# First head's values token by token, sample products in column strips, gates in one tile

## The chip, the cores and the metric

The kernel runs on one core of a Trainium2 chip. The metric is device time in microseconds of one launch; lower is better. The engines are called by their short names: PE multiplies matrices, DVE, ACT and POOL work on vectors, SP only issues transfers.

## What is computed

One inference step of a small hybrid layer: 512 new "prompt" frames without history and 32 "sample" frames that continue a stream with a stored state, 544 columns in all, model width 1024. The parts that matter here:

```python
xn = _rmsnorm(h, norm_g[l])
proj = xn @ w_in[l]
u, v_m, z_m, ig_pre, fg_pre, q_h, f_h, i_h, g_h, ga, gb = jnp.split(proj, _split_points(), axis=-1)
c = jax.nn.silu(_causal_conv(u, ...))            # 4 heads of 512 channels
qm, km = c @ w_qm, c @ w_km * M_HD ** -0.5       # per head
vm = v_m                                          # per head, 512 wide
ig, lf = ig_pre + b_ig, log_sigmoid(fg_pre + b_fg)
# mLSTM, per chunk and head
s = jnp.einsum('bhtd,bhsd->bhts', q, k) * dmat
num = w_inter[..., None] * jnp.einsum('bhed,bhtd->bhte', C, q) + jnp.einsum('bhts,bhse->bhte', s, v)
h = num / jnp.maximum(jnp.abs(den), jnp.exp(-m_t))[..., None]
C_new = decay[..., None, None] * C + jnp.einsum('bhs,bhse,bhsd->bhed', w_last, v, k)
...
hm = (_head_layernorm(h) + m_skip * c) * jax.nn.silu(z_m)
ya = hm @ w_brm
# a second branch (8 gated heads of 128), merge gates, w_out, and an output gate
```

The sample frames carry an old memory C (512 x 512 for each of the four heads); the prompt frames start from zero. Outputs are the layer's result and the new states of both streams, among them the memory C of each head (Cp for the prompt, Cs for the sample).

## The kernel before

**Precision.** An fp32 matrix is kept as a rounded high part and a rounded low part (fp32r), and a product is three PE instructions: high x high, low x high, high x low. The split of a weight is one copy (ACT, the high part) and one subtraction (DVE or POOL, the low part). Operands left as plain fp32 need one instruction for the exact product, which the profile shows as two records.

**Layout.** Work is feature-major: a tile has 128 features on the partitions and the 544 columns on the free axis, sample frames first, cut in two halves of 272. `dense` and `steps` go over the eight 128-row tiles of the contraction; with three parts and two halves, a unit of 128 output features is 48 PE instructions.

**The front.** PE first makes four units u (input of the convolution of head 0), then the two gates: `wg` has 36 columns, four at 0 for one gate and four at 32 for the other, and `steps(gp, wg, range(KD), 0, 36, 36)` is 48 products. Then `values()` makes four units v of head 0, with the low parts of their weights on POOL; each result is copied to a tile `vt`. Meanwhile DVE normalises x (`norm`, `norm_low`) and runs the convolution. The raw x and the raw weights stay in memory for a while; weights come in pieces of 512 columns, through a ring of eight raw buffers and a ring of five split pieces.

**The heads.** For each of the four heads in turn: keys (`stage_k`), queries (`stage_q`), scores (`stage_scores`: 512 x 512, and the sample's), then `mchain`, then the output projection (`stage_br`). `mchain` is a generator. It transposes the keys (blocks "kt", "kts"), loads the old memory c0 (four tiles), transposes the values (four blocks "vt" and the sample's "vts"), makes the new memory of the prompt (`memory`, tiles C, written out through Co), the numerators "nm" of the four row blocks, the numerators of the sample, the sample's new memory ("Cs", `new_memory`, eight pieces that are added to c0 by DVE), and the transposed result "yt". At each `yield n` it gives PE to a `Pump` for n steps of six instructions: the pump works through the input units that later stages need (z gates, values and u of the next head, the other branch's units) and prepares their weights a few pieces ahead. `EARLY` is the number of pump steps ahead of the first head's keys; a unit has eight.

**The sample block.** `old(f)` splits each of the four old memory tiles into high and low parts, and the query is split too. In `sample()` the query's high and low parts of several tiles stand side by side in the stationary operand (up to 128 columns), so that 18 products of 258 columns give the result in two strips of PSUM partitions, which are copied and added.

**The end.** The last head's new memory for the prompt does not lie in `mchain`: its operands go through DRAM, and `memories()` makes it at the very end of the kernel, in two PSUM banks of the other pool (`phalves`). The last tile's two copies to Co are followed by one transfer of the whole tile.

**Order.** The front's order on ACT, DVE and PE is the order of the code (`tc.manual_schedule`); after it only PE's is, and a scheduler places the instructions of the others; `tc.high_priority` and `tc.issue_after` move them ahead or hold them back. PSUM has eight banks: two two-bank buffers (`paux`) and four single ones (`pd`).

Of the kernel before, what the change touches and what calls it, by code (L numbers as in the profile page):

```python
# [46 lines left out]
AHEAD = 3  # L47
SCRATCH = 1024
# [3 lines left out]
EARLY = 8  # L52
# [12 lines left out]
def hybrid_step(ctx: ExitStack, tc: tile.TileContext, a, o):  # L65
# [69 lines left out]
    def weight(src, name, cols=1024, eng=V, chunk=WP):  # L135

        raws = [(raw_piece(src[:, c : min(c + WP, cols)], f"{name}r{c}"), min(WP, cols - c)) for c in range(0, cols, WP)]
        return [split_piece(r, f"{name}{i}", n, chunk, eng) for i, (r, n) in enumerate(raws)]

# [149 lines left out]
    cmask3 = cp.tile([3 * NS, NS], F32, name="cmask3")  # L289
    vone = cp.tile([3 * NS, 4], F32, name="vone")  # L290
# [557 lines left out]
    def stage_scores(h):  # L848

        dj, ds, wi, ks, ksm, qs, qf, qw = (st8[h][k] for k in ("dj", "ds", "wi", "ks", "ksm", "qs", "qf", "qw"))  # L850
        for i in range(KH):
            qt = small("qt", [P, NS])
            G.tensor_tensor(qt, qf[:, i * NS : (i + 1) * NS], wi, ALU.mult)
            G.tensor_copy(qw[:, i, 0], qt)
            G.tensor_tensor(qw[:, i, 1], qt, qw[:, i, 0].bitcast(F32), ALU.subtract)
# [40 lines left out]
    def memory(h, f, kw, vv, pool=paux):  # L896
# [16 lines left out]
        with tc.high_priority():  # L913
            for g in range(2):
                S.copy(co[:, g * VH : (g + 1) * VH], pn[g][:, :VH])  # L915
        nc.sync.dma_start(o["Cp"][h, f], co[:, :VW])
        yield

    kv_d = dr.tile([2 * NB, 2, P, VW], F32, name="kv_d")

    def mchain(h, pump):
# [23 lines left out]
        with tc.high_priority():  # L945
            S.mul(kws, pt[: 3 * NS, 0, :], wc)
            lo = slice(2 * NS, 3 * NS)
            V.scalar_tensor_tensor(kws[lo], pt[lo, 0, :], wc[lo], kws[lo].bitcast(F32), ALU.mult, ALU.subtract)
# [4 lines left out]
        def old(f):  # L953
            new = eslot if f < 2 else slot
            ch, cl = new(f"c0h{h}{f}", F32R), new(f"c0l{h}{f}", F32R)
            with tc.high_priority():
                S.copy(ch[:, :VW], c0[f][:, :VW])
                V.tensor_tensor(cl[:, :VW], c0[f][:, :VW], ch[:, :VW].bitcast(F32), ALU.subtract)
            return ch, cl


        if h:
            yield max(0, max(pump.when["v", f] for f in range(KH)) - pump.done)
        vt = t["vt"]
        vv = []
        for b in range(NB):
            yield 1
            pt = paux(f"vt{h}{b}")
            for f in range(KH):
                PE.transpose(pt[:, 0, f * P : (f + 1) * P], vt[f][:, NS + b * P : NS + (b + 1) * P], ident)  # L970
            if b < 2:
                vhl = sp.tile([P, 2, SLOT], F32R, tag="d", name=f"vhl{h}{b}", bufs=2)
# [937 lines left out]
```

## Time and profile before

| | |
|---|---|
| median of three runs | 1129.78 us (1127.34 to 1130.38) |
| the profiled execution | 1129.4 us, of which 1127.7 us are the span |
| PE busy | 1116.1 us (99%), 8849 records |
| DVE busy | 899.9 us (80%) |
| ACT busy | 682.4 us (61%) |
| POOL busy | 189.0 us (17%) |
| TensorE's granted clock | 1.0 throughout |
| memory traffic | 157.85 MB, 140 GB/s over the span |

A profile is one execution. Rows of the timeline and of the chain of waits have the start in us, the duration in us, the engine, the line, the operation with output and inputs, the size of the stationary operand (rows x columns) where it is a product, the shape, and the number of instructions in the row; a bracket behind tells a wait and what ended it. A record of PE is longer than the distance to the next one, because instructions overlap: distances are read from starts. In the view of waits a row gives the waiting operation, the releasing one, and then the total in us, the count and the longest. Groups give the count, the shape, and the lowest, middle and highest duration in ns, or the busy time with the mean, and then the idle time before. Rows of transfers end with the microseconds from issue to landing.

### The profile page before, as it was taken

The numbers are of one execution on the slowest core, as the hardware profiler recorded it, in microseconds if no ns is written. First come the engines' busy times: TensorE is split into PE (matmuls) and PEld (weight loads), VectorE is DVE, ScalarE is ACT, GpSimd is POOL, SyncE is SP. The second block draws the span as 40 slices with busy tenths as digits, with TensorE's granted clock in tenths as the row PEclk, the third lists the DMA queues.
The fourth block names the chain that finished last, engine by engine and source line by source line (L and its number), as shares of the span: only waits on it lengthen the run. The fifth ranks groups of instructions, "written<-read, shape, count | busy, mean of one in ns | idle before, by whom it ended". The sixth has DMA issues, their size and how long they took to land.

```text
span 1127.7 us, 24054 instructions
## 1 busy us (share of the span) xinstructions
PE 1116.1 (99%) x8849; PEld 1101.9 (98%) x8849; DVE 899.9 (80%) x2034; ACT 682.4 (61%) x1537; POOL 189.0 (17%) x356
## 2 busy tenths in 40 slices
PE   9999999999999999999999999999999999999998
PEld 9999999999999999999999999999999999999998
DVE  6886998576797786986888789999999977654585
ACT  5677657655666564665666477777776667332462
POOL 4842010100020100201000133232322210000000
PEclk9999999999999999999999999999999999999999
DMA  6133224323344142542667665666665685332743
GB/s 238 56 97 126 79 85 148 130 77 122 128 155 157 46 125 98 172 165 77 198 190 244 175 145 140 142 134 148 154 157 139 158 222 161 109 104 70 271 142 117
DMA packets 89997, 157.85 MB, mean 140 GB/s; under 512 B 10132, under 2 KB 17684, under 8 KB 89880
## 3 DMA queue, kind: packets, MB, share of 16 engines
q1 hardware_dynamic: 80928, 140.27, 38.4%
q0 software_dynamic: 8784, 15.99, 9.1%
q8 instruction: 69, 1.13, 0.4%
q14 instruction: 48, 0.39, 0.1%
q10 hardware_dynamic: 168, 0.06, 0.0%
HBM read 131.37 MB, written 24.91 MB: 139 GB/s over the span
## 4 chain that ended last, share of the span: by engine, by line
PE 85%; DVE 8%; DMA 3%; ACT 2%; issue 1%; POOL 0%; SPq 0%; ACTq 0%; DVEq 0%
PE d L485 35%; PE ya L151 9%; PE pg L1760 4%; PE q L151 4%; PE yb L151 4%; PE o L151 4%; PE C L903 4%; PE k L151 4%; PE sc L863 3%; PE pl L1532 2%; PE nm L1078 2%; DMA ws<-in_w_in 2%; PE ple L151 1%; DVE cv L634 1%; PE ht L1608 1%
## 5 line engine op out<-in xcount | busy, mean ns | idle before, releaser
L403 POOL DMA_DIRECT2D ws<-in_w_in x46 | 40.3, 877 | 239.9 <-DVE hkq L1556 36.7
L499 ACT COPY t<-d 128x272 f32<-128x272 f32 x126 | 47.8, 379 | 10.3 <-PE d L485 10.3
L1556 DVE TENSOR_TENSOR hkq<-hkq,q 128x288 f32<-128x288 f32 (+1 forms) x96 | 40.8, 432 | 3.5 <-ACT t L499 1.0
L634 DVE SCALAR_TENSOR_TENSOR cv<-ub,vec,cv 128x547 f32<-128x547 f32 x48 | 40.3, 840 | 1.7 <-ACT cv L629 1.4
L1532 PE MATMUL pl<-hkq,km 128*128 128x128 f32 x224 | 37.6, 290 | 1.3 <-ACT km L1521 1.2
L1532 PEld LDWEIGHTS pl<-hkq,km 128*128 128x128 f32 x224 | 31.2, 189 | 2.7 <-ACT km L1521 2.4
L1521 ACT COPY km<-hkq 128x256 f32<-128x256 f32 x56 | 24.0, 429 | 14.7 <-DVE hkq L1556 5.4
L1007 DVE SCALAR_TENSOR_TENSOR c<-c,wi,Cs 128x258 f32<-128x258 f32 x32 | 15.3, 479 | 20.1 <-PE Cs L1005 19.9
L915 ACT COPY Co<-C 128x258 f32<-128x258 f32 x32 | 10.4, 378 | 29.1 <-PE C L903 20.3
L1150 DVE TENSOR_TENSOR y<-ya,y 128x272 f32<-128x272 f32 x48 | 18.8, 434 | 8.8 <-PE ya L151 8.8
L1563 DVE COPY_PREDICATED at<-lmask,pl 128x256 f32<-128x256 uint8 (+1 forms) x56 | 25.2, 451 | 0.1
L626 POOL COPY uo<-ub 128x3 f32<-128x3 f32 x16 | 18.0, 1125 | 33.9 <-DVE ub L508 27.4
L1089 ACT COPY y<-nm 128x516 f32<-128x516 f32 x16 | 9.5, 591 | 21.6 <-PE nm L1078 21.6
L800 POOL COPY vsm<-vt 128x96 f32<-128x96 f32 x16 | 6.0, 384 | 88.2 <-ACT vt L510 44.7
L460 POOL DMA_DIRECT2D ws<-in_w_in x15 | 15.7, 1046 | 28.2 <-DVE ws272l L131 24.1
L1500 POOL TENSOR_SCALAR_AFFINE_SELECT aa<-at 128x128 f32<-128x128 f32 x32 | 18.4, 610 | 8.1 <-DVE at L1563 8.0
L1078 PE MATMUL nm<-vhl,sh 128*128 128x258 f32 x112 | 18.4, 286 | 0.0
L1037 DVE BATCH_NORM_STATS2 bs<-y 128x6 f32<-128x512 f32 (+1 forms) x20 | 13.7, 688 | 5.5 <-ACT y L1089 5.4
L979 POOL CAST vhl<-one 128x4 fp32r<-128x4 f32 x8 | 2.0, 245 | 95.8 <-PE nm L1078 95.8
L1747 DVE TENSOR_TENSOR h<-o,h 128x272 f32<-128x272 f32 x16 | 6.3, 436 | 14.5 <-PE o L151 14.5
L877 ACT CAST sh<-dm 128x512 fp32r<-128x512 f32 (+3 forms) x16 | 7.3, 459 | 16.6 <-DVE dm L871 16.6
L1662 ACT ACTIVATE osq<-kq 128x128 f32<-128x128 f32 x32 | 9.8, 305 | 12.4 <-DVE kq L1657 12.1
(4490 smaller groups left out, 5077.3 us busy)
## 6 DMA issues: line engine op xcount, KB each, us to landing
ws<-in_w_in POOLq DMA_DIRECT2D x61, 256.0 KB, 4.8
ws<-in_w_in SPq DMA_DIRECT2D x46, 256.0 KB, 3.8
ya_d<-y SPq DMA_DIRECT2D x32, 272.0 KB, 2.2
y<-ya_d SPq DMA_DIRECT2D x24, 272.0 KB, 3.8
c<-in_C SPq DMA_DIRECT2D x16, 258.0 KB, 4.0
out_Cp<-Co SPq DMA_DIRECT2D x16, 258.0 KB, 2.4
out_Cs<-c SPq DMA_DIRECT2D x16, 258.0 KB, 2.8
x<-in_xT SPq DMA_DIRECT2D x8, 272.5 KB, 4.8
```

The costliest lines, as they stand in the source:

```text
L151: PE.matmul(both[b][:m, :TH], part(w, off + k * step, m, x), xx[:, half(b)], start=(k == 0 and j == 0), stop=(k == n - 1 and j == 2),)
L403: G.dma_start(t, w_in[u][:, i * WP : (i + 1) * WP], accum_op=ALU.add)
L485: PE.matmul(ps, ww[:, c], xx, start=(start and k == 0 and j == 0), stop=end, skip_group_check=not start,)
L499: self.kept = S.copy(t, ps)
L634: V.scalar_tensor_tensor(cv[:, :547], ub[:, j : j + 547], vcol(V_CW + 4 * ft + j), cv[:, :547], ALU.mult, ALU.add)
L863: PE.matmul(pn[:, 0, :n], ks[f][x][:, j * P : (j + 1) * P], qs[f][y][:, NS + j * P : T], start=(f == 0 and i == 0), stop=(f == KH - 1 and ...
L903: PE.matmul(pn[g][:, :VH], kw[b][x][:, f * P : (f + 1) * P], vv[b][y][:, g * VH : (g + 1) * VH], start=(b == 0 and j == 0), stop=(b == NB ...
L1078: PE.matmul(pn[:, g, :VH], st[j][x][:, (i - j) * P : (i - j + 1) * P], vv[j][y][:, g * VH : (g + 1) * VH], start=(j == 0 and q == 0), stop ...
L1532: PE.matmul(pn[:, 0, b * P : (b + 1) * P], km[:, b * P : (b + 1) * P], view(qq, b * P, ((2 * c, P // (2 * c)), (HB + c, 2), (1, c))), star ...
L1556: V.tensor_tensor(x, x, d, ALU.mult)
L1563: V.copy_predicated(at[:, :n], lmask[:, li, :n], pn[:, 0, :n])
L1760: PE.matmul(ps, part(w, k * P, P, x), xx[:, c], start=(k == 0 and j == 0), stop=(k == KD - 1 and j == 2))
```

## The change

It has these parts.

- **Gates.** The gate weight is padded to 64 columns, and `gate_weight` builds one stationary tile of 100 columns out of it: the 64 rounded high ones and the 36 low ones. The high part of x meets all 100, the low part only the 36, so each of the eight contraction tiles takes two products for each half. The two gates come out in one tile `gt`, the low strip added by DVE.
- **Values of the first head.** They are made with the tokens on the partitions: x is the stationary operand (128 columns), the weight (512 columns, from a new arrangement `w_v` of the same numbers) the moving one; four PSUM banks `vp`, 96 products. The 32 sample rows are eight plain fp32 products `vq`: x times its norm weight (`xg`) against the raw weight, each in one of four strips of 32 output columns of PE, two deep. The row factor of the norm is applied by ACT and DVE as they read PSUM. So head 0 has no vt and vts transposes. The weights are split by ACT and DVE, not POOL, and DVE makes all low parts of x.
- **Sample block.** The query and c0 are used as plain fp32, without splits: for each half of the columns four products, one for each c0 tile, in four strips, and the product with the sample's own scores on top of the first. ACT copies one strip, DVE adds three. In the first three heads it stands ahead of the new memory; in the last one behind the first numerator block.
- **Memory.** The sample's new memory pieces are spread: one at each of four places in the numerators, the rest between pump steps of four ahead of yt. In the last head fewer pump steps stand before the first yt.
- **Front.** `EARLY` goes from 8 to 16: two z units ahead of the first keys. Small POOL operations are held behind one early sum (`issue_after(summed)`), sums `xf` are moved, the third convolution input is copied by ACT.
- **End.** The last memory tile is made, copied and sent by halves (`memory_halves`), on ACT's queue.

```diff
-EARLY = 8
+EARLY = 16
...
+    def gate_weight(src, name):
...
+            t = t[:, : n * (GW + GN)].rearrange("p (k c) -> p k c", k=n)
+            r = raw[:, i * n * GW : (i + 1) * n * GW].rearrange("p (k c) -> p k c", k=n)
+            S.copy(t[:, :, :GW], r)
+            V.tensor_tensor(t[:, :, GW:], r[:, :, :GN], t[:, :, :GN].bitcast(F32), ALU.subtract)
...
-            t.update(qs=[], qf=small("qf", [P, KH * NS]), qw=small("qw", [P, KH, 2, NS], F32R))
+            t.update(qs=[], qf=small("qf", [P, KH * NS]), qw=small("qw", [P, KH, NS]))
...
-    def memory(h, f, kw, vv, pool=paux):
+    def memory(h, f, kw, vv, pool=paux, after=None):
...
-        nc.sync.dma_start(o["Cp"][h, f], co[:, :VW])
+        (nc.scalar if pool is phalves else nc.sync).dma_start(o["Cp"][h, f], co[:, :VW])
...
+    def memory_halves(h, f, kw, vv, pn):
+
+        co = eslot(f"Co{h}{f}")
+        for g in range(2):
+            c = slice(g * VH, (g + 1) * VH)
...
+            S.copy(co[:, c], pn[g][:, :VH])
+            nc.scalar.dma_start(o["Cp"][h, f][:, c], co[:, c])
...
-        def old(f):
-            new = eslot if f < 2 else slot
-            ch, cl = new(f"c0h{h}{f}", F32R), new(f"c0l{h}{f}", F32R)
+        if h == 0:
+            vv, vs = t["vv"], t["vs"]
+        else:
...
-        yield 4
-        olds = [old(0), old(1)]
+                xf[1] = xf_sums(1)
+        yield 3
...
+        def sample():
+            pn = paux(f"nm{h}{NB}")
+            for g in range(2):
+                v = slice(g * VH, (g + 1) * VH)
+                for f in range(KH):
+                    PE.matmul(pn[f * NS : (f + 1) * NS, g, :VH], qw[:, f], c0[f][:, v], start=True, stop=f > 0)
+                PE.matmul(pn[:NS, g, :VH], dss, vs[:, v], start=False, stop=True)
+            ysm = eslot(f"y{h}{NB}")
+            with tc.high_priority():
+                first = S.copy(two(ysm[:, :VW]), pn[:, :, :VH])
+                for f in range(1, KH):
+                    last = V.tensor_tensor(
+                        two(ysm[:NS, :VW]), pn[f * NS : (f + 1) * NS, :, :VH], two(ysm[:NS, :VW]), ALU.add
+                    )
+            return ysm, first, last
...
-                if parts and i and (h == MH - 1 or i > 1):
+                if parts and (i, j) in ((1, 1), (2, 1), (3, 0), (3, 2)):
                     new_memory(*parts.pop(0))
...
+            if i == 0 and h == MH - 1:
+                ysm, *_ = sample()
+                numbers(NB, NS, ysm)
...
-            yield max(GAP if f == 0 else 1, pump.when["z", f] - pump.done)
+            while parts:
+                yield 4
+                new_memory(*parts.pop(0))
+            yield max(GAP - (16 if h == MH - 1 else 0) if f == 0 else 1, pump.when["z", f] - pump.done)
...
-            (V if k % 2 else G).tensor_tensor(xs[k][1], xt[k][:, :T], xs[k][0].bitcast(F32), ALU.subtract)
-
+            V.tensor_tensor(xs[k][1], xt[k][:, :T], xs[k][0].bitcast(F32), ALU.subtract)
...
-        steps(gp, wg, range(KD), 0, 36, 36)
...
+        vp = [pd.tile([P, 512], F32, tag="h", name=f"vp{b}") for b in range(NB)]
+        vq = paux("vq")
...
+            three = ((xh, wh), (xl, wh), (xh, wl))
+            for b in range(NB):
+                for j, (x, w) in enumerate(three):
+                    PE.matmul(
+                        vp[b],
+                        x[:, NS + b * P : NS + (b + 1) * P],
+                        w,
...
+            if k % NB == NB - 1:
+                for j in range(NB):
+                    i = k + 1 - NB + j
+                    PE.matmul(vq[j * NS : (j + 1) * NS, 0, :], xg[:, i], wraw[i], start=(i < NB), stop=(i >= NB))
...
+        def value_out():
...
+            c = r[:, b + 1 : b + 2]
+            S.mul(vh[:, :HD], vp[b], c)
+            V.scalar_tensor_tensor(vl[:, :HD], vp[b], c, vh[:, :HD].bitcast(F32), ALU.mult, ALU.subtract)
...
-        for f in range(KH):
+        for f in range(KH - 1):
             yield from memory(MH - 1, f, kw, vv, phalves)
+        memory_halves(MH - 1, KH - 1, kw, vv, phalves(f"C{MH - 1}{KH - 1}"))
+        yield
```

The first place is ACT between the end of the first head's values and the first keys, before. wi32 and wi33 are the weight pieces of the first two z units (two pieces each, 0 and 1), wk00 the first key weight, c and cs3h the convolved input, vt the values, z the z unit's silu.

```order
L1312 CAST cs2h<-c_905 128x544
L1303 COPY vt_915<-v_831 128x272
L1303 COPY vt_915<-v_832 128x272
L640 ACTIVATE c_968<-cv_667 128x32
L641 ACTIVATE c_968<-cv_667 128x512
L1312 CAST cs3h<-c_968 128x544
L130 CAST wi321h<-wi32r_893 128x512
L130 CAST wk000h<-wk00r_981 128x512
L130 CAST wk001h<-wk00r_983 128x512
L130 CAST wi330h<-wi33r_895 128x512
```

The same place on ACT in the changed kernel; vh are the value tiles, vp their PSUM banks.

```order
L1396 ACTIVATE vh_863<-vp_627,rms_r 128x512
L1396 ACTIVATE vh_869<-vp_628,rms_r 128x512
L657 ACTIVATE c_876<-cv_720 128x32
L658 ACTIVATE c_876<-cv_720 128x512
L688 ACTIVATE z_973<-z_973 128x544
L1381 CAST cs3h<-c_876 128x544
L132 CAST wi330h<-wi33r_818 128x512
L132 CAST wi331h<-wi33r_820 128x512
L132 CAST wk000h<-wk00r_895 128x512
L132 CAST wk001h<-wk00r_897 128x512
```

Before, the silu of the first z unit comes ten rows further down, behind wi330h and wi331h; now it stands ahead of cs3h and of the second unit's weights, and those stand ahead of the key weights.

The second place is PE at the sample block, before: the first seven of its eighteen products and the product with the sample's own scores (dss, vs). c0h and c0l are the parts of an old memory tile, qw the queries.

```order
L1055 MATMUL nm_2077<-c0h_1856,qw 128x258
L1055 MATMUL nm_2077<-c0l_1857,qw 32x258
L1055 MATMUL nm_2077<-c0h_1856,qw 128x258
L1055 MATMUL nm_2077<-c0l_1857,qw 32x258
L1055 MATMUL nm_2077<-c0h_1860,qw 64x258
L1055 MATMUL nm_2077<-c0l_1861,qw 32x258
L1055 MATMUL nm_2077<-c0h_1860,qw 64x258
...
L1052 MATMUL nm_2077<-vs,dss 32x258
```

The same block on PE now, whole; c are the four old memory tiles as loaded.

```order
L1041 MATMUL nm_1701<-c_1647,qw 32x258
L1041 MATMUL nm_1701<-c_1648,qw 32x258
L1041 MATMUL nm_1701<-c_1649,qw 32x258
L1041 MATMUL nm_1701<-c_1650,qw 32x258
L1042 MATMUL nm_1701<-vs,dss 32x258
L1041 MATMUL nm_1701<-c_1647,qw 32x258
L1041 MATMUL nm_1701<-c_1648,qw 32x258
L1041 MATMUL nm_1701<-c_1649,qw 32x258
L1041 MATMUL nm_1701<-c_1650,qw 32x258
L1042 MATMUL nm_1701<-vs,dss 32x258
```

Eighteen rounded products of 32 to 128 stationary columns became eight plain fp32 products and two rounded ones, all of 32.

More of the change, by code (lines that the diff above doesn't have):

```diff
@@ L1299, in values_out @@
[L1299 to L1306 removed]
+        norm_low(0)
+        with tc.issue_after(summed.ins):
+            uin.append(conv_in(3, acc[3], True))
+        value_weight()
+        cv = [conv_first(0, uin[0])]
+        gp = phalves("gates")
@@ L1356, in hybrid_step @@
             if h == 0:
+                with tc.issue_after(st8[0]["last"].ins):
+                    for k in (0, 3):
+                        xf[k] = xf_sums(k)
                 col, cols, combo = stage_cols(*rows)
```

309 lines of the change are left out of this document (175 added, 134 removed).

## The prediction

> **What bounds the kernel now.** First the page: which engine is full, and how much of the chain that ended last is its own.
>
> ```profile
> span 1127.7 us, 24054 instructions
> PE 1116.1 (99%) x8849; PEld 1101.9 (98%) x8849; DVE 899.9 (80%) x2034; ACT 682.4 (61%) x1537; POOL 189.0 (17%) x356
> PE 85%; DVE 8%; DMA 3%; ACT 2%; issue 1%; POOL 0%; SPq 0%; ACTq 0%; DVEq 0%
> ```
>
> TensorE (PE) is the bound. A busy share of 99% could hide gaps, since a record is longer than the step to the next one; so next the view of waits, for PE alone. All that it lists comes to 7 us:
>
> ```profile
> PE pl L1532 <- ACT km L1521: 1.2, 3, 0.7
> PE Cs L1005 <- DVE c L1007: 1.0, 3, 0.5
> PE vt L970 <- DVE vhl L978: 0.9, 1, 0.9
> PE yt L1120 <- DVE c L1128: 0.7, 1, 0.7
> PE r0pb L232 <- DVE rms_s L215: 0.3, 1, 0.3
> ```
>
> So the time is the number of PE steps times the step, plus a few waits. A change gains by taking steps off PE, and loses by new holes in PE. The steps are read from starts (timeline and chain), never from the length of a record:
>
> ```profile
> 177.79 24.16 PE ya L151 x192
> 227.38 0.40 PE L863 MATMUL sc<-qh,kh 128*128 128x512 f32 x1
> 230.16 0.34 PE L863 MATMUL sc<-qh,kh 128*128 128x384 f32 x1
> 33.98 0.66 PE L271 MATMUL gates<-x,wg0h 128*36 128x272 f32 x4
> 39.17 0.66 PE L271 MATMUL gates<-x,wg0h 128*36 128x272 f32 x4
> ```
>
> A rounded product with 272 columns costs 24.16/192 = 0.126 us. Between the 227.38 and the 230.16 row lie twelve products of 512 columns: 0.232 each. From the first gate row to the last named one are seven contraction tiles of six products: 5.19/42 = 0.124.
>
> **The change part by part.** *Gates:* 32 products instead of 48: -16 x 0.124 = -2.0 us.
>
> *First head's values, prompt:* 192 products of 272 columns go (-24.2), 96 of 512 come (+22.3): -1.9 us.
>
> *Values' transposes:* four blocks "vt" and one "vts" of the first head go.
>
> ```profile
> 117.26 0.41 PE L370 MATMUL d<-xh,wi340l 128*128 128x272 f32 x2
> 118.57 0.63 PE L970 MATMUL vt<-ident,vt 128*128 128x128 f32 x4 [0.89 <-DVE vhl L978]
> 118.95 0.50 PE L370 MATMUL d<-xh,wi340h 128*128 128x272 f32 x2
> 119.29 0.41 PE L370 MATMUL d<-xl,wi340h 128*128 128x272 f32 x2
> ```
>
> A block takes 118.95 - 118.57 = 0.38, and the pair of rounded products behind it 0.34 where 0.25 is usual: 0.47 a block, five blocks -2.4 us. The one long wait, 117.26 to 118.57 less 0.25, goes too: -1.1. But what DVE did there stays: preparing weights of the next units and the sums xu. Behind the scores DVE has six such operations of about 0.65 between its parts of the four kt blocks, so I expect kt and kts to wait about 1.2 in its place. Net: -2.3.
>
> *Sample values and sample strips.* Both use true f32 products, two PE records each, in four strips of 32 output partitions. Nothing in this trace has strips beside each other. The price of an f32 record, from a place with 128 columns:
>
> ```profile
> 667.83 1.05 PE L1627 MATMUL su<-hi,hkq 128*128 128x128 f32 x8
> 668.72 0.39 PE L1628 MATMUL su<-kit 128*128 128x128 f32 x2
> 668.86 0.37 PE L485 MATMUL d<-xh,wa1250h 128*128 128x272 f32 x1
> ```
>
> Eight records in 0.89 us: 0.111. That may be the weight load of 128 columns or the stream. If it is the stream, 258 columns cost 0.224 and 512 columns 0.444; if it is the load, 0.120 and 0.232 as for rounded ones. I take the dearer, since two passes per record fit the 0.111 either way, and keep the cheaper for the range. Before, the sample block is:
>
> ```profile
> 287.15 0.29 PE L1055 MATMUL nm<-c0h,qw 128*128 128x258 f32 x1
> 287.28 0.28 PE L1055 MATMUL nm<-c0l,qw 128*32 128x258 f32 x1
> 287.40 0.28 PE L1055 MATMUL nm<-c0h,qw 128*128 128x258 f32 x1
> 289.20 0.28 PE L1055 MATMUL nm<-c0h,qw 128*128 128x258 f32 x1
> 289.32 0.65 PE L1078 MATMUL nm<-vhl,sh 128*128 128x258 f32 x4
> ```
>
> 18 products in 2.17 us. After: per half four strips (8 records) and one rounded product. With strips side by side a half lasts as its one strip, 2 x 0.224, and the block 4 x 0.224 + 2 x 0.12 + 0.17 for two returns from f32 (0.085 each, as behind vt) = 1.3: -0.87 a head, -3.5 us. One record after the other it is 16 x 0.224 + 0.41 = 4.0, +1.8 a head. The eight sample value products cost 4 x 0.444 = +1.8 side by side, 16 x 0.444 = 7.1 in a row. I take side by side: each strip has weights and output partitions of its own.
>
> The rows 287.15 to 287.40 also show that going between 128 and 32 stationary columns costs nothing, 0.12 a step. The Trainium skill, "TensorEngine Tiling (Array Packing)", Key Properties, says that a change of tiling mode drains TensorE; by it the change would pay a drain at either end of each strip group, while here the trace disagrees at the first strip, and no row shows the others. The Trainium skill, "TensorE: Matmul & The Clock Gate", What overlaps and what doesn't, has matmuls in strict order of start and end, and measured 2.38 times the speed for three column tiles; by that the sample block would lie between my two ends.
>
> *What DVE and ACT do for it.* The splits of the old memory (a copy and a subtraction, sixteen of each) go; both engines have slack there, so nothing on PE is counted but half a microsecond of waits like yt's: -0.5. Two more additions of strips per head come on DVE (three for one), a PSUM buffer's release waiting on them:
>
> ```profile
> L993 DVE TENSOR_TENSOR vs<-vts,vs x4: 684/684/685, 121.2 to 566.9; 32x512 fp32r<-32x512 f32 x4
> L1089 ACT COPY y<-nm 128x516 f32<-128x516 f32 x16 | 9.5, 591 | 21.6 <-PE nm L1078 21.6
> ```
>
> 0.59 + 3 x 0.68 + hand-overs = 2.9 us. In heads 0 to 2 a pump step (0.76) and a memory product (24 x 0.12 = 2.9) run meanwhile. In the last head only nm1 does (12 products and one Cs, 1.6): PE waits +1.2. Spreading the Cs products takes the 1.0 of waits on c away. In the first head two old-memory tiles are loaded only behind the last kt block; three pump steps and the first strips cover all but +0.4.
>
> *The hole between the first two z units.* EARLY = 16 puts the second z unit ahead of the keys. Before, its first weight piece wi330h is copied on ACT ahead of the first unit's silu; now behind it, with cs3h between. PE needs wi330h, and the silu needs the first unit's end:
>
> ```profile
> 72.22 0.78 DVE L669 COPY z<-d 128x272 f32<-128x272 f32 x2
> 75.37 0.66 ACT L671 ACTIVATE z<-z 128x544 f32<-128x544 f32 x1
> 65.81 0.65 ACT L1312 CAST cs3h<-c 128x544 fp32r<-128x544 f32 x1
> 67.92 0.62 ACT L130 CAST wi330h<-wi33r 128x512 fp32r<-128x512 f32 x1
> ```
>
> 0.78 + 0.66 + 0.65 + 0.62 and 0.2 of hand-overs: PE stands still +2.9 us. Queued behind wi330h are wi331h and the first key weights, which then have a whole unit (6 us) of cover.
>
> *Start.* The second half of wu3 and the gate weights now stand behind the reciprocal root on DVE: r0pb's 0.3 goes. Two of the four value banks are the gates' own: they wait for two copies and additions behind DVE's norms, +0.6. DVE takes over the subtractions of the value weights and of x that POOL did beside it:
>
> ```profile
> 30.12 2.17 DVE L1255 SCALAR_TENSOR_TENSOR x<-x,rb 128x544 f32<-128x544 f32 x3
> 36.05 2.44 DVE L1255 SCALAR_TENSOR_TENSOR x<-x,rb 128x544 f32<-128x544 f32 x2
> ```
>
> 0.72 each at 30 us, 1.22 where POOL subtracts at the same time. With POOL idle, DVE at 0.7 keeps ahead: I count some 30 operations, 21 us, for the 25 us of value products that cover them. If that cover fails, rival 3 has the price.
>
> *Tail.* The last memory tile by halves:
>
> ```profile
> 1123.59 0.65 ACT L915 COPY Co<-C 128x258 f32<-128x258 f32 x2 [2.23 <-PE C L903]
> out_Cp<-Co SPq DMA_DIRECT2D x16, 258.0 KB, 2.4
> out_y<-h SPq DMA_DIRECT2D x16, 136.0 KB, 1.8
> ```
>
> One copy (0.38 for 0.65) and a transfer of half the size (1.8 for 2.4) stand behind PE's end: -0.9.
>
> *Sum:* -2.0 - 1.9 - 2.3 + 1.8 - 3.5 - 0.5 + 1.2 - 1.0 + 0.4 + 2.9 - 0.3 + 0.6 - 0.9 = -5.5 us. The profiled execution took 1129.4 (1127.7 of span and 1.7 around it), so 1123.9; the median of the runs, 1129.8, lies 0.4 higher: 1124.3.
>
> **The rivals.** *1. The strips chain* (the change does not quite do what it says). The two records of one f32 product use the same strip, so the second waits for the first, and in order of issue only it and the next strip's first overlap: five lengths for four strips. Sample values 10 x 0.444 = 4.4 (+2.6), sample block 9 x 0.224 + 0.41 = 2.4 (+1.1, four times): -5.5 + 2.6 + 4.4 = +1.5, 1131.3. For it: records come in pairs, and PE starts them in order. Against it: a cheap f32 record (0.120, 0.232) brings the same chain back to about 1125.
>
> *2. The strips do not overlap at all*, at the sample values and in every head: sample values +5.3 over my sum, blocks +2.7 four times: +10.6, 1140.4, slower. It decides once a block takes over about 3.6 us. For it: no row has two products at once. Against it: the separate output partitions.
>
> *3. The front starves.* DVE's operations stay at 1.2 instead of 0.7 while PE multiplies the first values; twelve operations more than fit, each 0.5, PE waits 6 us before z: +0.5, 1130.3; with the hole growing alike, 1133. For it: 36.05 above. Against it: POOL has only small copies left.
>
> **How the numbers follow.** The forecast's case 0.58, rival 1 0.24, rival 2 0.10, rival 3 0.08. A measurement of this kernel tells 0.3% from no change, 3.4 us. The first case is faster by more than that in nine of ten; rival 1 splits 0.2 faster, 0.5 the same, 0.3 slower; rival 2 is slower; rival 3 is 0.3 the same, else slower. Faster 0.52 + 0.05 = 0.57, same 0.06 + 0.12 + 0.02 = 0.20, slower 0.07 + 0.10 + 0.06 = 0.23. The range's lower end is my sum with cheap f32 records (-2.6) and no hole and no waits at kt (-4.1): -12.2, 1117.5. Its upper end is rivals 1 and 3 with 2.5 for unknown waits: 1134. Left out are rival 2 and the outer part of the others. The first case alone has 1118 to 1128.
>
> **What would show it.** In the profile after: the starts of the eight vq products and of a head's strips (1.3, 2.4 or 4.0 us a block decide between the cases); PE waiting on ACT wi330h for about 2.9; PE waiting on y in the last head for 1.2; vp products 0.232 apart without waits on DVE; the span ending about 3.2 behind PE's end. I am wrong if vp waits for its weights, if the keys start more than 4 us later than the removed and added products say, or if a strip block costs over 3.6.

## The result, and the profile after

The changed kernel takes 1135.62 us (median of five runs, 1134.34 to 1137.21), the kernel before 1129.78 (median of five too, 1127.34 to 1130.38): a ratio of 1.0057, 95% interval 1.0043 to 1.0072. It is slower by 6 us, where 5.5 us less were forecast. Each later ratio is to executions of the kernel before that were timed beside it, with medians between 1128.85 and 1129.23 us. The page and the cores' view (span and mean granted clock) of the changed kernel:

```profile
span 1133.3 us, 23757 instructions
PE 1112.4 (98%) x8733; PEld 1088.1 (96%) x8733; DVE 900.9 (79%) x2040; ACT 669.5 (59%) x1506; POOL 163.7 (14%) x308
PE 83%; DVE 5%; DMA 3%; ACT 2%; issue 1%; POOL 0%; ACTq 0%; POOLq 0%; DVEq 0%
core 0: 1133.3 us, clock 0.995
```

PE has 116 records fewer, and they are done later. Two things are new: a granted clock below 1, and in the waits of PE (waiting line, releaser, then us in total, count, longest) holes that before had no like:

```profile
PE C L917 <- ACT Co L929: 3.8, 1, 3.8
PE d L387 <- ACT wi330h L132: 2.5, 1, 2.5
PE k L167 <- POOL wk010l L133: 1.3, 1, 1.3
PE u L287 <- DVE wf2l L133: 1.3, 1, 1.3
PE nm L1094 <- ACT y L1105: 1.2, 2, 0.7
PE k L167 <- ACT wk010h L132: 1.0, 1, 1.0
```

Set side by side, the starts of PE's stages in the two timelines give a ledger (us):

| stretch of PE | before | after | after minus before |
|---|---|---|---|
| start of the gates | 33.98 | 35.24 | +1.3 |
| gates | 5.94 | 3.99 | -1.9 |
| values up to the first z | 24.09 | 25.13 | +1.0 |
| z units (one, now two) | 6.48 | 16.21 | +9.7 |
| first keys | 13.63 | 16.40 | +2.8 |
| rest of the first head, up to its "ya" | 93.51 | 90.49 | -3.0 |
| heads two, three, four | 428.11 | 423.89 | -4.2 |
| last "ya" to the last memory | 504.59 | 505.46 | +0.9 |
| last memory to the end of the span | 17.34 | 16.51 | -0.8 |

The second z unit (6.0 us) is only moved: it belongs to the rest of the first head, which so loses 3.0 and not gains. The first 188 us lose 9.8 us, the three later heads and the tail give 5.0 back, and 0.9 is lost in the long middle part, which has the same products before and after. In the profiles of this case that part takes 503.6 to 506.7 us, so 0.9 is within its spread.

### The profile page after: what moved, and what is told of

It reads as the page before. It is cut to its first block, busy times and chain, and to the rows that moved or that the text cites. A ratio compares the mean times of both kernels' runs of the same rounds, so it can differ in the third digit from the quotient of the medians.

```text
span 1133.3 us, 23757 instructions
## 1 busy us (share of the span) xinstructions
PE 1112.4 (98%) x8733; PEld 1088.1 (96%) x8733; DVE 900.9 (79%) x2040; ACT 669.5 (59%) x1506; POOL 163.7 (14%) x308
## 4 chain that ended last, share of the span: by engine, by line
PE 83%; DVE 5%; DMA 3%; ACT 2%; issue 1%; POOL 0%; ACTq 0%; POOLq 0%; DVEq 0%
PE d L502 34%; PE ya L167 8%; PE yb L167 4%; PE q L167 4%; PE o L167 4%; PE pg L1860 4%; PE k L167 4%; PE C L917 4%; PE sc L877 3%; PE nm L1094 3%; PE pl L1632 2%; DMA ws<-in_w_in 2%; PE ple L167 1%; PE yt L1142 1%; PE ht L1708 1%
## 5 line engine op out<-in xcount | busy, mean ns | idle before, releaser
L651 DVE SCALAR_TENSOR_TENSOR cv<-ub,vec,cv 128x547 f32<-128x547 f32 x48 | 37.5, 783 | 0.4
L917 PE MATMUL C<-vhl,kwh 128*128 128x258 f32 x96 | 16.5, 296 | 4.4 <-ACT Co L929 3.8
L917 PEld LDWEIGHTS C<-vhl,kwh 128*128 128x128 f32 x96 | 14.0, 201 | 4.7 <-ACT Co L929 4.0
L1094 PEld LDWEIGHTS nm<-vhl,sh 128*128 128x128 f32 x112 | 15.4, 190 | 2.0 <-ACT y L1105 1.7
```

Of the source, the lines that this page charges most:

```text
L651: V.scalar_tensor_tensor(cv[:, :547], ub[:, j : j + 547], vcol(V_CW + 4 * ft + j), cv[:, :547], ALU.mult, ALU.add)
L917: PE.matmul(pn[g][:, :VH], kw[b][x][:, f * P : (f + 1) * P], vv[b][y][:, g * VH : (g + 1) * VH], start=(b == 0 and j == 0), stop=(b == NB ...
L1094: PE.matmul(pn[:, g, :VH], st[j][x][:, (i - j) * P : (i - j + 1) * P], vv[j][y][:, g * VH : (g + 1) * VH], start=(j == 0 and q == 0), stop ...
```

## The experiments

**The hole at the memory.** The longest wait stands between the second and the third tile of the first head's new memory. First PE's timeline there, then ACT's:

```profile
137.07 0.28 PE L1027 MATMUL Cs<-vs,kws 96*128 96x258 f32 x1
141.17 1.23 PE L917 MATMUL C<-vhl,kwh 128*128 128x258 f32 x4 [3.82 <-ACT Co L929]
145.55 0.28 PE L1027 MATMUL Cs<-vs,kws 96*128 96x258 f32 x1
```

```profile
139.76 0.43 ACT L340 ACTIVATE xfh<-xv 128x272 fp32r<-128x272 f32 x1
140.47 0.65 ACT L929 COPY Co<-C 128x258 f32<-128x258 f32 x2 [0.28 <-DMA out_Cs<-c]
144.58 0.65 ACT L929 COPY Co<-C 128x258 f32<-128x258 f32 x2 [3.14 <-DMA out_Cp<-Co]
```

PSUM is not free because Co has not been copied; the copy's own releaser is a transfer that writes out an old-memory tile. Either the copy has no buffer until that tile is gone, or it stands behind the casts xfh in ACT's queue. By the code, the ring of twelve buffers ("e") then holds three z tiles, four value parts, four old-memory tiles and the sample's y. One edit frees a tile earlier and leaves the casts:

```diff
+            if h == 0:
+                new_memory(*parts.pop(0))
+                new_memory(*parts.pop(0))
             for f in range(KH):
                 for _ in memory(h, f, kw, vv, after=read):
```

> The changed kernel with one edit: in the first head two pieces of the sample's new memory (both halves of the first old-memory tile) stand ahead of the prompt's memory, so that this tile is written out and its buffer comes free earlier. Theory A (buffers): PE stands still 3.98 us at 137 us because the first Co has no free buffer until the first old-memory tile has been written out; with the edit that hole and the half clock behind it (1.5 us more) go, about -5 us, 1130.5. Rival B (order on ACT): Co stands behind the casts of the sums xf, which wait for DVE; DVE is as late as before, so the hole stays and the time is 1135.6 within 1.

1128.88 us, a ratio to the kernel before of 0.9993 (0.9983 to 1.0003). The first Co is copied at 133.1 us, and PE's stretch from the first C to "ya" falls from 57.07 to 51.06 us. Theory A holds: 6 us of the loss come from a missing buffer, the 4.0 us hole and the slow products behind it.

The products behind that hole are slow, too. The windows view (busy PE, count, granted clock, DMA share, GB/s) around the three long holes:

```profile
72.00:72.50 0.50, 0.00 (x0) 1.00 0.00 0
72.50:73.00 0.50, 0.00 (x0) 0.63 0.00 0
73.00:76.00 3.00, 2.84 (x12) 0.50 0.34 87
76.00:77.00 1.00, 1.00 (x10) 0.98 0.32 84
89.50:90.00 0.50, 0.11 (x1) 0.70 0.00 0
90.00:93.00 3.00, 3.00 (x13) 0.50 0.43 105
93.00:94.00 1.00, 1.00 (x9) 0.95 0.60 215
140.50:141.00 0.50, 0.00 (x0) 0.90 0.00 0
141.00:144.00 3.00, 2.83 (x13) 0.50 0.49 175
144.00:145.00 1.00, 1.00 (x9) 0.85 0.00 0
```

From the last half us of each hole the granted clock is half for 3.4 us: a mean of 0.63 over the first half us is 0.37 us at half clock, then come 3.0 and then 0.04, and the other two add up alike. In the kernel before, no hole was that long, and the clock was 1.0 until PE's last product. The Trainium skill, "TensorE: Matmul & The Clock Gate", Part 1, tells of such a gate, with free-running windows of 3.4 us. The traces agree on the length: ahead of PE's last product, every stretch at half clock in these runs lasts 3.4 us or twice that. The next run tests whether the idle time is the cause.

```diff
                 new_memory(*parts.pop(0))
+                if h == 0 and f == 1:
+                    fillp = pd.tile([P, 512], F32, tag="h", name="fillp")
+                    for _ in range(14):
+                        PE.matmul(fillp, kw[0][0][:, :P], vv[0][0][:, :512], start=True, stop=True)
```

> The changed kernel with fourteen products added in the memory's hole at 137 us (512 columns, 0.232 us each, 3.25 us in all, into a PSUM bank that nothing reads). They need only what is there, so they run while PE would wait for the first Co. Theory A (clock): the granted clock drops because PE stood still, and the 3.4 us at half speed behind the hole go once it is filled: the third memory tile's twenty-four products take 2.9 us instead of 4.5, the mean granted clock rises by about 0.0015, -1.5 us, 1134. Rival B: the slow stretch behind the hole is something else (transfers, weights, a refill of queues): no change, 1135.6, or longer where the products delay the memory.

1135.34 us, ratio 1.0049 (1.0036 to 1.0062): not to be told from the changed kernel's. PE's timeline, where fillp are the added products:

```profile
137.95 3.44 PE L1072 MATMUL fillp<-vhl,kwh 128*128 128x512 f32 x14
141.96 0.74 PE L917 MATMUL C<-vhl,kwh 128*128 128x258 f32 x4 [0.57 <-ACT Co L929]
144.96 0.28 PE L1027 MATMUL Cs<-vs,kws 96*128 96x258 f32 x1
146.11 0.75 PE L917 MATMUL C<-vhl,kwh 128*128 128x258 f32 x4 [0.87 <-ACT Co L929]
```

The clock stayed at 1.00, and the third tile's 24 products took 3.0 us for 4.4. All six kernels of this case that keep the hole, the changed one among them, show the half clock there, so the idle time is its cause. But the fourth tile now waits 1.0 us: each Co copy waits for the transfer of the one before it, as in ACT's rows above, and the slow clock had only hidden that wait. From the first C to the first "yt" it is 42.7 us for 42.8. Theory A is right on the clock and wrong on the time.

**The holes of the front.** Behind the hole of the z units, PE waits twice at the second key weight, wk010. PE's timeline, then ACT's ahead of that weight's copy, both in the changed kernel:

```profile
87.82 0.52 PE L167 MATMUL k<-cs0h,wk010h 128*128 128x272 f32 x2 [1.05 <-ACT wk010h L132]
89.89 0.60 PE L167 MATMUL k<-cs0h,wk010l 128*128 128x272 f32 x1 [1.30 <-POOL wk010l L133]
```

```profile
80.82 1.28 ACT L726 ACT_TABLE_LOAD   x1
82.79 1.28 ACT L688 ACT_TABLE_LOAD   x1
84.08 0.66 ACT L688 ACTIVATE z<-z 128x544 f32<-128x544 f32 x1
84.76 1.28 ACT L727 ACT_TABLE_LOAD   x1
87.17 0.60 ACT L132 CAST wk010h<-wk01r 128x512 fp32r<-128x512 f32 x1
```

The copy comes 6.6 us after the keys' start (80.57). In the kernel before it came 3.0 us after it (70.49), ahead of the silu and its table load:

```profile
73.45 0.60 ACT L130 CAST wk010h<-wk01r 128x512 fp32r<-128x512 f32 x1
```

Waits in the text are gaps between PE's starts less one step; the idle time in a row's bracket is 0.1 to 0.3 us shorter. Four edits follow, each on the changed kernel: the second z unit's first weight ahead of other work; the silu of the first z unit behind the key weights' copies; the second key weight at high priority; POOL's small copies no longer held behind the early sum.

```diff
         conv_rest(2, uin[2], cv[2])
-        silu_low(1)
         silu()
         conv_rest(3, uin[3], cv[3])
         value_out()
         value_out()
+        pump.prepare(5)
+        silu_low(1)
         silu_low(2)
         silu()
-        pump.prepare(5)
```

> The changed kernel with one edit: the first weight piece of the second z unit (wi330) is prepared ahead of the last convolved input and of the low parts cs1l and cs2l. Theory A: the hole between the first two z units (2.66 and 0.27 us of waiting, and 1.0 us of the half clock behind it) goes: -3.7 us, 1131.9. Rival B: DVE and ACT are the bound of this stretch, and what is won there is waited for again at the keys, whose weights come from the same queues: within 1 us of 1135.6, the keys' waits longer by 3 us.

```diff
-            act = S.activation(z[:, :T], z[:, :T], AF.Silu)
+            with tc.issue_after(made["wk001"][0].ins) if f == 0 else nullcontext():
+                act = S.activation(z[:, :T], z[:, :T], AF.Silu)
```

> The changed kernel with one edit: the silu of the first z unit is held behind the copy of the key weight wk001 on ACT, so that it no longer stands ahead of cs3h, wi330h, wi331h and wk000h. Theory A: the hole between the first two z units is ACT's order and nothing else; without the silu wi330h is copied about 1.9 us earlier, the wait falls from 2.66 to under 1 us, the clock stays full, and the silu falls behind the table loads of the gate rows so that one of them goes as well and the key waits shrink: -3 to -6 us in all, 1130 to 1132.5. Rival B: what is won is given back at the keys, as it was when only the weight was moved ahead: 1135 to 1143.

```diff
-            w = st8[h].pop("wk", None) or weight(a["w_km"][h, u], f"wk{h}{u}", eng=V if h else G)
+            with tc.high_priority() if u and not h else nullcontext():
+                w = st8[h].pop("wk", None) or weight(a["w_km"][h, u], f"wk{h}{u}", eng=V if h else G)
```

> The changed kernel with one edit: the second key weight is prepared with high priority, so that its copy on ACT stands ahead of a table load, a silu and the key copies. Theory A: the two key waits (1.21 and 1.46 us) and the half clock behind them (about 1.5 us) come from ACT's queue; -3 to -4 us, 1132. Rival B: POOL's subtractions of the low parts (1.3 to 2.0 us each) are the bound, and the second wait stays: -1 us, 1134.6.

```diff
-        with tc.issue_after(summed.ins):
-            uin = [conv_in(f, acc[f], False) for f in range(NF)]
+        uin = [conv_in(f, acc[f], False) for f in range(NF)]
...
-            with tc.issue_after(summed.ins):
-                G.tensor_copy(vh[:, HD:VW], one4)
-                G.tensor_copy(vl[:, HD:VW], zero4)
+            G.tensor_copy(vh[:, HD:VW], one4)
+            G.tensor_copy(vl[:, HD:VW], zero4)
```

> The changed kernel with one edit: the small copies on POOL are not held behind the early sum any more (xg still is), so that POOL's second addition of squares comes after them, as before the change. Theory A: this addition, beside DVE's subtraction of wf2, stretched that to 1.86 us from 0.55 and made PE wait 1.4 us; it goes: -1.3 us, 1134.3, wf2l at 0.6 us. Rival B: PE waits there for x and the first weights, which landed 0.6 us later in this execution: no change beyond 0.5 us.

| run | median, us | ratio to before (95%) | keys begin | first queries begin | scores begin |
|---|---|---|---|---|---|
| changed kernel | 1135.62 | 1.0057 (1.0043 to 1.0072) | 80.57 | 96.97 | 110.58 |
| z_weight_ahead | 1143.67 | 1.0134 (1.0109 to 1.0159) | 78.92 | 99.51 | 118.55 |
| z_silu_late | 1132.51 | 1.0032 (1.0020 to 1.0044) | 78.14 | 96.28 | 109.99 |
| key_weight_ahead | 1136.47 | 1.0064 (1.0042 to 1.0087) | 79.92 | 93.39 | 108.69 |
| pool_fill_free | 1133.43 | 1.0043 (1.0028 to 1.0058) | 77.99 | 96.95 | 110.58 |

The last three columns are PE's starts in the profiled executions. Each edit closed its own hole, and most of it was waited for again before the scores. z_weight_ahead lost more than it won: PE then waited for the key weight wk011 3.4 and 2.4 us, and for a query 3.0 us, and ran at half clock for 6.8 us behind the keys' waits and again behind the query's; what rival B names, and worse. In z_silu_late the wait for wi330h fell to 0.8 us as theory A has it, but the keys then waited 2.1 us for a PSUM bank, as rival B has it. In key_weight_ahead the second key wait went too, against its rival B; then PE waited 1.1 us for a bank and 1.4 us for a query weight, and the time is the changed kernel's. In pool_fill_free the wait for wf2l went, against its rival B, and the gates start 1.60 us earlier, but the first queries 0.02. So the local mechanism was right in all four, and the time followed it only in part. In pool_fill_free the keys begin 2.6 us earlier, and all of it is lost up to the first queries: PE waits 2.1 us for wk010h instead of 1.2, and the half clock behind the key waits lasts 6.8 us instead of 3.4. z_silu_late (at the edge of its theory A) and pool_fill_free (below its own) were timed 3 and 2 us faster than the changed kernel although their scores begin no more than 0.6 us earlier, but the interval of each touches that of the changed kernel. For z_silu_late its single executions give a likely reason: the profiled execution (1135.55 us) has two stretches of 6.8 us at half clock and a mean clock of 0.993, while the other four ran at 0.997 or 0.998 and took 1131.83 to 1132.74.

EARLY back at 8:

> The changed kernel with EARLY back at 8, the keys straight behind the first z unit. Theory A: the keys' weights stand behind the same silu and the same copies on ACT and then behind POOL's subtractions, so PE waits for the first key weight about 5 us instead of 2.7 for wi330h, and the second z unit no longer covers the rest: slower than the changed kernel by 2 to 5 us, 1137.5 to 1140.5. Rival B: the second z unit ahead of the keys is itself the harm, and the time goes back by the hole and its clock, -3.7, to 1132.

1129.60 us, ratio 1.0002 (0.9993 to 1.0011). Theory A had the front right: PE waits 3.7 us for the first key weight and 2.8 us for a query weight. It missed the memory: with one z tile less in the ring, the 4 us hole is not there, which shows the missing buffer a second time. Rival B's time is nearer, but not for the reason it gives, the hole between the z units and its clock.

**The strips.** PE's timeline of the sample block in the changed kernel, the four parts of each product merged:

```profile
128.12 0.64 PE L1041 MATMUL nm<-c,qw 128*32 128x258 f32 x8
128.69 0.30 PE L1042 MATMUL nm<-vs,dss 96*32 96x258 f32 x1
128.93 0.64 PE L1041 MATMUL nm<-c,qw 128*32 128x258 f32 x8
129.50 0.31 PE L1042 MATMUL nm<-vs,dss 96*32 96x258 f32 x1
129.65 0.41 PE L387 MATMUL d<-xh,wi350h 128*128 128x272 f32 x2
```

Eight records in 0.57 us; the block takes 1.53. To see what lying side by side is worth, all four products go to one strip, on the kernel with the buffer mended:

```diff
-                    PE.matmul(pn[f * NS : (f + 1) * NS, g, :VH], qw[:, f], c0[f][:, v], start=True, stop=f > 0)
+                    PE.matmul(pn[:NS, g, :VH], qw[:, f], c0[f][:, v], start=(f == 0), stop=False)
```

> The kernel of mem_two_ahead (1128.9), with the four old-memory products of each half of the sample block all in one strip of 32 columns, added up in PSUM, without DVE's additions. Theory A: the strips run side by side, and in one strip the sixteen records of a block follow each other at 0.111 to 0.24 us: a block takes 3.0 to 4.3 us for 1.6, four heads +6 to +10, less 1 us of waits for DVE's additions: 1134 to 1138. Rival B: the records would be as quick one after the other, and the strips only cost the additions: 1128 or less.

1137.10 us, ratio 1.0069 (1.0056 to 1.0083), 8 us more than mem_two_ahead. The same eight records:

```profile
127.93 1.93 PE L1041 MATMUL nm<-c,qw 128*32 128x258 f32 x8
129.79 0.31 PE L1042 MATMUL nm<-vs,dss 96*32 96x258 f32 x1
```

1.86 us for 0.57: four strips run 3.3 times as fast as one strip. Theory A holds.

**What is left when the holes are closed.** four_mended joins mem_two_ahead, z_silu_late, key_weight_ahead and pool_fill_free; key_copies_first adds high priority for the copies of the first keys out of PSUM; key_lows_on_DVE puts those key weights' subtractions on DVE; early_8_mended has EARLY 8 with the key and POOL edits alone.

> The changed kernel with four edits together: two pieces of the sample's new memory ahead, small POOL copies free, the second key weight at high priority, the first silu of z held back. Theory A: the holes were the whole loss (5.3 + 1.4 + 4 + 3.7 us of the span, some of it counted twice because a later wait takes it over): 1122 to 1126, faster than the kernel before by 4 to 7 us. Rival B: DVE, 90% busy from 60 to 100 us, is the bound of the front, so that only the memory's hole is won: 1128 to 1130.

> four_mended (1126.4) with the copies of the first keys out of PSUM at high priority, ahead of a table load and the gate rows on ACT. Theory A: PE's wait of 2.64 us for a PSUM bank at 83 us and the half clock behind it are this order on ACT; they go, part of it is waited for again at the next weight: -1.5 to -3 us, 1123.4 to 1125. Rival B: DVE and POOL are the bound, no change: 1126.4.

> key_copies_first with the subtractions of the first head's key weights on DVE, not POOL. While POOL subtracts (1.3 to 1.8 us each), DVE's operations of the same kind take 1.8 us instead of 0.69. Theory A: POOL's help costs DVE as much as it saves; with all four on DVE (4 x 0.69 = 2.8 us) DVE loses about 2.5 us of stretching and the weights are ready earlier: same as key_copies_first or up to 1.5 us faster. Rival B: DVE is full and four more operations delay all that stands behind them: +1 to +3 us over key_copies_first.

> The changed kernel with EARLY 8, small POOL copies free, the second key weight and the key copies at high priority, and without the two pieces of memory ahead. Theory A: with EARLY 8 no hole at the memory is there, since one z tile less holds a buffer, but the first keys wait 3.7 us for wk000h whatever stands behind, and the clock drops there: 1127 to 1129, slower than key_copies_first by 2 to 5 us. Rival B: the order of units does not matter once the buffers are free: as key_copies_first within 1 us.

| run | median, us | ratio to before (95%) | scores begin |
|---|---|---|---|
| four_mended | 1126.37 | 0.9978 (0.9969 to 0.9988) | 107.33 |
| key_copies_first | 1126.09 | 0.9969 (0.9958 to 0.9980) | 108.03 |
| key_lows_on_DVE | 1125.87 | 0.9973 (0.9964 to 0.9982) | 107.40 |
| early_8_mended | 1131.33 | 1.0014 (1.0005 to 1.0022) | 107.02 |

With the memory's hole gone and one table load less, four_mended is faster than the kernel before, by 2.5 us, which is 0.4 us short of its theory A's range. After that the scores begin at 107 to 108 us whatever is closed; in key_copies_first PE waits for DVE's wq001l (2.7 us) instead of the keys' bank, and the time stays, as its rival B has it. key_lows_on_DVE is level with key_copies_first, as its theory A has it. early_8_mended is 5.2 us slower than key_copies_first, a little more than its theory A has it. It was also timed slower than early_8, though its profiled execution is 1.2 us shorter in span; that stays open.

DVE is the engine named in that wait. The windows of all engines from the first gate to the first score, before and after (PE, PEld, DVE, ACT and POOL busy, then granted clock, DMA share and GB/s):

```profile
33.98:97.83 63.85, 62.85 (x503) 61.20 (x501) 52.95 (x86) 46.20 (x101) 37.08 (x48) 1.00 0.34 105
```

```profile
35.24:110.58 75.34, 70.29 (x456) 62.34 (x455) 66.95 (x128) 52.16 (x105) 15.22 (x28) 0.95 0.30 93
```

DVE is busy 14 us longer there, POOL 22 us shorter. Part of it are the sums xf(0) and xf(3), put ahead of the scores by the change. The next two kernels put them back, on the changed kernel and on key_copies_first:

```diff
-                with tc.issue_after(st8[0]["last"].ins):
-                    for k in (0, 3):
-                        xf[k] = xf_sums(k)
...
                 with tc.issue_after(low.ins):
+                    for k in (0, 3):
+                        xf[k] = xf_sums(k)
                     lower_bounds()
```

> The changed kernel with the sums xf(0) and xf(3) behind the first head's scores, where they were before the change. Each is eleven operations on DVE (about 4.9 us) and three on ACT (1.5 us). Theory A: DVE bounds the first head's front (67 of 75 us busy from the gates to the scores, for 53 of 64 before), and these 9.8 us are the largest thing that was put ahead of the scores; without them the scores start 2 to 4 us earlier, and the time falls by as much: 1131.5 to 1133.5. Rival B: they then stand ahead of the key transposes' parts and are waited for there: within 1 us of 1135.6.

> key_copies_first (1126.1, five edits) with the same sums behind the scores. Theory A: PE's wait of 2.65 us for wq001l on DVE and the slow clock behind it go, and the kernel comes to 1122 to 1124.5. Rival B: 1126 within 1, the wait shifted to the key transposes.

On the changed kernel the scores begin at 110.62, no earlier. Its 1133.28 us (ratio 1.0039, 1.0027 to 1.0052) are inside its theory A's range, but the interval overlaps the changed kernel's, and the profiled execution reaches "ya" no earlier; it gains only in the middle part, within that part's spread. With the other holes closed the scores begin at 105.71 for 108.03, the clock is 1.000, and the time is 1124.42 (ratio 0.9955, 0.9942 to 0.9967). Theory A of the second holds in time and clock, though the wait for wq001l only shrank, from 2.7 to 1.9 us; that of the first falls in its mechanism: the sums delay the scores only once the queues ahead of them are in order.

Last, the parts: the change's heads and tail on the kernel before, and the same with the gate tile.

> The kernel before with the change's heads and tail alone: sample block in strips and ahead of the memory, spread memory pieces, last memory by halves. The front, the gates, the first head's values and EARLY 8 stay as before. Theory A: this is where the change gains (heads 1 to 3: 1.4, 1.0 and 1.8 us, the last memory 0.9, and about 1 in the first head) and the front is where it loses: 1129.1 - 6.1 = 1123. Rival B: in the first head the memory's copies find no buffer here either, as at 137 us in the changed kernel: 1127 to 1129.

> heads_only with the gates in one tile, 32 products for 48. Theory A: the 16 products are saved on PE and nothing stands behind them: -2 us on heads_only, 1121. Rival B: the front is bound by DVE and ACT, which make the normalised x and the value weights that PE needs next; PE waits for them as much longer: as heads_only within 0.5 us.

heads_only: 1124.26 us, ratio 0.9965 (0.9952 to 0.9979), clock 1.000, no hole at the memory: rival B falls, and theory A is 1.3 us short. Its first "ya" lies 1.4 us earlier than before, its last one 4.6, the end of its span 5.1. heads_and_gates: 1125.11 us, ratio 0.9963 (0.9950 to 0.9975), not to be told from heads_only. There PE's timeline in the values is:

```profile
44.07 0.41 PE L167 MATMUL v<-x,wv01l 128*128 128x272 f32 x2
45.52 0.51 PE L167 MATMUL v<-xh,wv10h 128*128 128x272 f32 x2 [1.04 <-ACT wv10h L132]
46.91 0.39 PE L167 MATMUL v<-xh,wv10l 128*128 128x272 f32 x1 [0.62 <-POOL wv10l L133]
```

The gates are 1.95 us shorter and the values behind them 2.2 us longer: what the 16 products save is waited for again at once, as rival B has it.

heads_only, without the new front, and xf_late_mended, with all of the change and its queues mended, end level. So, as far as these two kernels tell, the gain of some 5 us is that of the heads and the tail, and the new front adds nothing to it even when its queues are mended.

## Why the prediction was wrong

The ledger and the sum are some 11 us apart: the rest of the first head 5.9, the first keys 2.8, the start 1.6, the middle part 0.9, the hole between the z units 0.8 and the values 0.5 worse than counted, the later heads 1.4 better.

- *Gates, -2.0:* measured -1.9. *Values, -1.9, +1.8 for the sample rows, +0.6:* +1.0 for +0.5; a group of four sample products takes 0.99 us with its returns, where 0.89 was counted, and the wait for gt is 0.2.
- *Sample strips, -3.5:* side by side, as taken; a block 1.53 for 1.3, since the step of each dss product is 0.24 and 0.15 and 0.09 is lost ahead of it. The later heads gain 4.2 in all (Cs waits gone, the last head's wait for y 0.7 for 1.2) where about 2.8 was counted. *Values' transposes, -2.3:* they are gone, and of the 1.2 us counted against them 0.6, at kts, was waited for. *Tail, -0.9:* -0.8.
- *The hole between the z units, +2.9:* the place, the releaser and the wait (2.7 us) are as worked out. Missing was the half clock: the stretch lost 3.7.
- *The start, -0.3:* r0pb's wait went, but the weight wf2l, stretched on DVE from 0.55 to 1.86 us beside POOL's addition, and 0.6 us later data made the gates start 1.3 later. The prediction gave no cost to holding POOL's copies behind the early sum; in pool_fill_free, without that, the gates start 1.60 us earlier.
- *The step that failed in the front* is "Queued behind wi330h are wi331h and the first key weights, which then have a whole unit (6 us) of cover". The first key weight had it. The second, wk010, stood behind three table loads, two rows and a silu on ACT, and then behind POOL's subtraction, which the sum did not count. PE waited 2.7 us and lost 1.7 to the half clock behind it, 4.4 in all, where this stage lost 1.6 in the kernel before: +2.8.
- *The step that failed in the first head* is the old-memory line, "three pump steps and the first strips cover all but +0.4". It counted loads, and those were covered, but asked for no buffers. Four value parts and one z tile more hold five of the twelve buffers: the hole of 4 us, the stretch 6 us too long. This is the largest term, but not the whole miss: mem_two_ahead, without it, is level with the kernel before and not 5.5 us faster. DVE's additions of the strips, taken as covered in this head, made PE wait 0.7 us once.
- *The rivals.* 1 and 2 fell: no chain in the strips. 3 asked the right question in the wrong place: the first values did not wait for DVE (vp products 0.23 apart, but for 0.2 us at the start), the stages behind them did.

What was not seen as a whole: the front's vector work was taken as cover with slack ("I count some 30 operations, 21 us, for the 25 us"), counted for the values alone. From gates to scores DVE was 83% busy before and 89% after. In this stretch most of what an edit closed came back as the next wait; that DVE's load as a whole is the reason is a reading of these runs, and no run tests it by itself.

## What to carry to other kernels

When a change keeps a tile alive longer or starts a stage sooner, count the buffers of its ring at the fullest moment as carefully as the instructions: a copy without a buffer stops the engine that is otherwise never idle. Where vector engines are near full for a stretch, price the stretch by their work and follow each queue to the last operation PE needs; closing one hole there only shows the next. Price a long wait on PE with the slow clock behind it, and ask what that slow stretch hides.

## What the runs showed of the hardware

- Ahead of PE's last product, the half clock came in stretches of 3.4 us or 6.8 us in every trace that has it. Behind the 4 us hole it came in all six kernels that keep the hole, and with the hole filled the clock stayed at 1.00.
- For shorter holes the length alone does not decide. The same hole of 2.7 us between the z units led to half clock in five kernels and not in hole_filled and pool_fill_free; the wait of 1.4 us for wf2l led to it in z_weight_ahead and not in the changed kernel; a hole of 1.9 us in xf_late_mended did not.
- Four fp32 products in four strips of 32 columns start within 0.02 us of each other, their second passes 0.22 us later (258 columns) or 0.44 (512): eight records in 0.57 us against 1.86 in one strip.
- A DVE subtraction of a weight piece took 0.69 us alone and up to 1.8 us while POOL subtracted another; in the kernel before POOL paid instead, with 2.4 us for 1.4. Yet moving those POOL operations to DVE changed the time by nothing that could be measured.
